# Float32 projection in fp32r halves: where the sum of two weight blocks is formed

## The chip, the cores and the metric

The kernel runs on one core of one Trainium2 chip. The metric is the device time of one execution in microseconds. Several runs are made, and their median counts. Besides, one execution is recorded by the hardware profiler; its trace says what each engine did at what time.

## The reference

One layer of a decoder trunk: a sequence of 1024 tokens with 2048 features each. A combined projection is followed by two groups of heads (sparse attention on a latent, and a chunked matrix memory), an output projection and a normalisation. The change lies in the combined projection. Cut to what matters:

```python
def reference(x, w_in, ..., w_out, ln_g, ln_b):
    ...
    proj = x @ w_in[l]                       # (1024, 2048) @ (2048, 7512), float32
    (q_a, c_kv, z_a, q_i, k_i, w_i, q_m, k_m, v_m, i_m, f_m, o_m, z_m) = jnp.split(proj, offs, axis=-1)
    ...
    y = jnp.concatenate([y_a, y_m], axis=-1) @ w_out[l]
    x = layer_norm(ALPHA * x + y, ln_g[l], ln_b[l])
```

## The kernel before

**Halves.** A float32 product is made of three matmuls of a shorter type (fp32r): each operand is split into a high part (a cast by ScalarE) and a low part (what is left, a subtraction by VectorE), and high times high, low times high and high times low are summed in PSUM.

**Seven products for eight.** The large part of the projection is not computed block by block. A product of two 2 x 2 block matrices is made of seven block products instead of eight. The blocks of the input X and sums of them are called a11, a12, a22, s1, s2, s3, s4; those of the weights b11, b21, b22 and the sums t1 to t4. With B(q, n) for the weight block of row half q (four k tiles of 128) and column n (128 columns), the code needs b11 = B(0, 0), b21 = B(1, 0), b22 = B(1, 1); t1 is made from B(0, 0) and B(0, 1); t2 is t1 and B(1, 1); t4 is t2 and B(1, 0); t3 is made from B(1, 1) and B(0, 1). (Signs are carried by the X sums and by the way in which results are added; the weight sums are plain additions here.)

**Units and passes.** Class `Unit` (from line 695) computes two column groups of 128 columns for all 1024 tokens. There are 20 units (NU), and the 2048 features are done in two passes of 1024: the first pass (second is False) stores its results in part_d, the second (second is True) loads them and adds. So there are 40 unit runs, each of seven products; a product is twelve matmuls of 128 x 512 (four k tiles, three matmuls each, line 754). A block of weights is 128 x 512 float32, 256 KB.

**The order around the change.** `unit(i, ...)` calls `begin` of the next unit (its product b11) ahead of `end` of this one (product t4); `middle` runs b21, t1, t2, b22, t3. In the code's order b11 of a unit is thus followed by t4 of the unit before, then b21 and t1; the first unit of a pass has no such t4. The planner of the build (a timeline simulation with its own estimates of costs) then places the instructions on the engines by priority; everything in `urgent()` has a raised priority. Each engine and each queue takes its instructions in the order that the planner wrote.

**Loads and buffers.** `Unit.load(q, n, more)` (line 715) takes a buffer wraw, starts a load of B(q, n) into it from the SP queue (line 720) and, where `more` names a second block, an accumulating load of it into the same buffer from POOL (line 723). It keeps the buffer in a dictionary under (q, n, more), so that a second request for the same key gives the same buffer. There are six wraw buffers (WR), four each for the high and low parts wh and wl (WB), shared by all users of those names. `weights(name)` (line 727) asks for the block, adds a second block on VectorE where needed (line 741), casts the high part on ScalarE (line 744) and subtracts the low part on VectorE (line 745). Before the change t1 is formed by its own pair of loads, under the key (0, 0, (0, 1)):

```python
                else:
                    src = self.load(0, 0, (0, 1))
                    if name != "t1":
                        vec.tensor_tensor(src, src, self.load(1, 1 if name == "t2" else 0), op=OP.add)
```

So t2 and t4 are formed in place in t1's buffer. A unit run loads five blocks over SP (b11, b21, t1's first, b22, t3's first) and two by accumulation over POOL (t1's and t3's second).

**What else runs beside the units.** In the first pass index matmuls (lines 577 and 578), their ScalarE and VectorE steps (579, 584) and a search for thresholds (615, 618); in the second pass the matrix memory (mLSTM), with a selection on POOL (line 996). PSUM results of a unit are added to the tile res by VectorE (line 763) or copied by ScalarE (765, 767).

Of the kernel before, what the change touches and what calls it, by code (L numbers as in the profile page):

```python
# [15 lines left out]
OP = mybir.AluOpType  # L16
# [86 lines left out]
def kernel(ctx, tc, a, out):  # L103
    nc = tc.nc
    vec, act, pool, pe, sync = nc.vector, nc.scalar, nc.gpsimd, nc.tensor, nc.sync
# [29 lines left out]
    def urgent():  # L135
        return tc.high_priority(offset=W_PRIO)
# [159 lines left out]
    class Queries:  # L296
# [3 lines left out]
        def run(self, p, again, X, between=lambda k: None):  # L300
# [35 lines left out]
            def product(ps, wname, xname, start, then):  # L336
                fh, fl = X[xname]
                for u in range(4):
                    wh, wl = weights(wname, u)
                    for k in range(4):  # L340
                        for n, (w, x) in enumerate(((wh, fh), (wh, fl), (wl, fh))):
                            last_mm[0] = pe.matmul(ps[u], w[:, k], x[:, k], start=start and k == 0 and n == 0,
                                                   stop=k == 3 and n == 2, skip_group_check=True)
                        if k % 2:
                            marks.append(last_mm[0])
                    then(u, ps[u])
# [326 lines left out]
    def search_on():  # L673

        if searching[0]:
            with tc.issue_after(last_cast[0].ins), tc.issue_after(last_low[0].ins):
                next(steps, None)
# [17 lines left out]
    class Unit:  # L695
# [31 lines left out]
        def weights(self, name):  # L727

            with urgent():
                if name == "b11":  # L730
                    src = self.load(0, 0)
                elif name == "b21":
                    src = self.load(1, 0)
                elif name == "b22":
                    src = self.load(1, 1)
                elif name == "t3":
                    src = self.load(1, 1, (0, 1))
                else:
                    src = self.load(0, 0, (0, 1))
                    if name != "t1":  # L740
                        vec.tensor_tensor(src, src, self.load(1, 1 if name == "t2" else 0), op=OP.add)  # L741
                wh = wp.tile([P, 4, P], F32R, name="wh", tag="wh", bufs=WB)
                wl = wp.tile([P, 4, P], F32R, name="wl", tag="wl", bufs=WB)
                last_cast[0] = act.copy(wh, src)  # L744
                last_low[0] = vec.tensor_tensor(wl, src, wh.bitcast(F32), op=OP.subtract)  # L745
            search_on()
            return wh, wl

# [66 lines left out]
    class Values:  # L815
# [11 lines left out]
        def run(self, second, X):  # L827
# [28 lines left out]
            def product(ps, wname, xname, start, group=4):  # L856
                fh, fl = X[xname]

                def part(t, k, w):
                    ts = slice(t * P, (t + 1) * P)  # L860
                    for n, (x, y) in enumerate(((fh, w[0]), (fl, w[0]), (fh, w[1]))):
                        last_mm[0] = pe.matmul(ps[t], x[:, k, ts], y, start=start and k == 0 and n == 0,
                                               stop=k == 3 and n == 2, skip_group_check=True)
                    if t % 2:
                        marks.append(last_mm[0])

                ws = {}
                for t0 in range(0, 4, group):
                    for k in range(4):
                        if not t0:  # L870
                            ws[k] = weights(wname, k)
                        for t in range(t0, t0 + group):
                            part(t, k, ws[k])
# [388 lines left out]
    with ExitStack() as ph:  # L1262
# [126 lines left out]
        for h in range(H_A):  # L1389
            qk = k_next + q_next  # L1390
            gt, tb = head_inputs(h) if h else head_0
            if h == 0:
                sync.dma_start(gt, gate_a[0])
            if h + 1 < H_A:
                k_next, q_next = keys(h + 1), queries(h + 1)
            order = range(4) if h < H_A - 1 else range(3, -1, -1)
            for n, p in enumerate(order):
                pr = weights(p, qk, tb)
                for step in y_steps.get(4 * h + n, ()):
                    y_step(*step)  # L1400
                consume(AHEAD - 1)
                if n == 0 and h % 2 == 0:
                    while blocks:
                        mix(blocks.pop(0))
                    values_of[h // 2] = values(h // 2)
                units.append((h, p, pr, gt, n == 3))
# [268 lines left out]
```

## Time and profile before

| | |
|---|---|
| median of 3 runs | 1823.08 us (1821.39 to 1825.92) |
| profiled execution | 1821.88 us |
| its span | 1820.1 us |
| TensorE busy (matmuls) | 1771.6 us, 97% |
| VectorE, ScalarE, GpSimd busy | 1398.2, 942.2, 267.7 us |
| loads of wg into wraw | 224 over SP, 80 over POOL |

In a row of the profile an engine has a short name: PE is TensorE (PEld its weight loads), DVE VectorE, ACT ScalarE, POOL GpSimd, SP SyncE; a q behind it (SPq) means its queue, which issues transfers and waits on semaphores. A group's row gives the line of the kernel, engine, operation, output<-inputs with shapes and xcount, then busy time and the mean in ns, then the idle time of the engine just before, and what ended most of it. A row of the timeline begins with start and duration in us; brackets at its end give the idle time before it and its releaser. A row of the waits gives, behind the two sides, the total in us, how many times, and the longest. A row of the stages begins with from:to, then the length in us, then each engine's busy time and instructions, the granted TensorE clock, the busy share of the DMA engines and GB/s. A DMA row gives KB each and the median us from issue to landing.

### The profile page before, as it was taken

The numbers are of one execution on the slowest core, as the hardware profiler recorded it, in microseconds if no ns is written. First come the engines' busy times: TensorE is split into PE (matmuls) and PEld (weight loads), VectorE is DVE, ScalarE is ACT, GpSimd is POOL, SyncE is SP. The second block draws the span as 40 slices with busy tenths as digits, with TensorE's granted clock in tenths as the row PEclk, the third lists the DMA queues.
The fourth block names the chain that finished last, engine by engine and source line by source line (L and its number), as shares of the span: only waits on it lengthen the run. The fifth ranks groups of instructions, "written<-read, shape, count | busy, mean of one in ns | idle before, by whom it ended". The sixth has DMA issues, their size and how long they took to land. (4 is left out here: it accounts for less than half of the span.)

```text
span 1820.1 us, 25472 instructions
## 1 busy us (share of the span) xinstructions
PE 1771.6 (97%) x8613; PEld 1492.9 (82%) x8613; DVE 1398.2 (77%) x2674; ACT 942.2 (52%) x1728; POOL 267.7 (15%) x324
## 2 busy tenths in 40 slices
PE   8999999999999999999999999999989999999997
PEld 8888888887888887788888887878788987788886
DVE  8756677767887768887878787877898976676787
ACT  6442266556666658322555565565665664333410
POOL 3101100000100010000101010010454530011000
PEclk9999999999999999999999999999999999999999
DMA  9994264445475657886766656475776447864764
GB/s 322 329 334 120 91 167 120 110 125 144 132 207 146 169 161 243 284 248 192 205 174 181 206 143 200 105 206 172 239 201 159 119 111 221 282 192 120 190 190 142
DMA packets 147069, 336.73 MB, mean 185 GB/s; under 512 B 15977, under 2 KB 25449, under 8 KB 140793
## 3 DMA queue, kind: packets, MB, share of 16 engines
q1 hardware_dynamic: 119576, 275.96, 45.8%
q0 software_dynamic: 27360, 59.13, 17.1%
q8 instruction: 68, 1.11, 0.2%
q14 instruction: 65, 0.52, 0.1%
HBM read 257.31 MB, written 91.35 MB: 192 GB/s over the span
## 5 line engine op out<-in xcount | busy, mean ns | idle before, releaser
L754 PE MATMUL pj<-xh,wh 128*128 128x512 f32 x960 | 375.8, 393 | 4.6 <-DVE res L763 3.8
L754 PE MATMUL pj<-xl,wh 128*128 128x512 f32 x960 | 374.9, 391 | 0.0
L754 PE MATMUL pj<-xh,wl 128*128 128x512 f32 x960 | 370.8, 391 | 0.6 <-DVE wl L745 0.6
L744 ACT CAST wh<-wraw 128x512 fp32r<-128x512 f32 x280 | 172.1, 619 | 203.0 <-PE pj L754 88.2
L745 DVE TENSOR_TENSOR wl<-wraw,wh 128x512 fp32r<-128x512 f32 x280 | 191.3, 687 | 46.6 <-ACT wh L744 40.9
L754 PEld LDWEIGHTS pj<-xh,wh 128*128 128x128 f32 x960 | 180.3, 188 | 43.0 <-ACT pqh L108 2.4
L754 PEld LDWEIGHTS pj<-xh,wl 128*128 128x128 f32 x960 | 180.1, 188 | 37.6 <-DVE wl L745 1.8
L754 PEld LDWEIGHTS pj<-xl,wh 128*128 128x128 f32 x960 | 180.4, 188 | 34.5
L723 POOL DMA_DIRECT2D wraw<-wg x80 | 68.1, 851 | 751.9 <-DMA wraw<-wg 254.5
L763 DVE TENSOR_TENSOR res<-res,pj 128x512 f32<-128x512 f32 x160 | 109.2, 682 | 53.7 <-PE pj L754 43.2
L584 DVE SCALAR_TENSOR_TENSOR sc<-r,wi,sc 128x384 f32<-128x384 f32 (+2 forms) x90 | 84.1, 948 | 30.9 <-ACT r L579 30.2
L579 ACT ACTIVATE r<-sc 128x384 f32<-128x384 f32 (+3 forms) x160 | 79.2, 523 | 52.3 <-PE sc L578 41.2
L615 ACT ACTIVATE junk<-sc,cand 128x512 bf16<-128x512 f32 (+2 forms) x93 | 86.7, 933 | 6.0 <-DVE cand L630 6.0
L108 ACT CAST wh<-wraw 128x512 fp32r<-128x512 f32 (+2 forms) x80 | 45.2, 571 | 70.4 <-PE lps L1487 22.0
L618 DVE TENSOR_SCALAR_CACHE_REDUCE junk<-sc,cand 128x384 bf16<-128x384 f32 (+2 forms) x93 | 80.0, 875 | 0.9
L1319 POOL TENSOR_TENSOR nm<-mask,tb 128x256 f32<-128x256 bf16 (+3 forms) x64 | 66.5, 1119 | 83.2 <-DVE mn L1326 76.8
L109 DVE TENSOR_TENSOR wl<-wraw,wh 128x512 fp32r<-128x512 f32 (+2 forms) x80 | 51.0, 642 | 30.3 <-ACT wh L108 28.6
L754 PE MATMUL pb<-xh,wh 128*128 128x512 f32 x160 | 62.9, 393 | 0.0
L754 PE MATMUL pb<-xh,wl 128*128 128x512 f32 x160 | 62.5, 391 | 0.0
L754 PE MATMUL pb<-xl,wh 128*128 128x512 f32 x160 | 62.4, 390 | 0.0
L1331 ACT ACTIVATE lg<-lg,mn 128x256 f32<-128x256 f32 (+3 forms) x64 | 50.4, 790 | 15.9 <-DVE mn L1326 15.9
L741 DVE TENSOR_TENSOR wraw<-wraw 128x512 f32<-128x512 f32 x80 | 55.0, 687 | 1.0
(562 smaller groups left out, 4476.6 us busy)
## 6 DMA issues: line engine op xcount, KB each, us to landing
wraw<-wg SPq DMA_DIRECT2D x224, 256.0 KB, 4.0
wraw<-wg POOLq DMA_DIRECT2D x80, 256.0 KB, 5.1
part_d<-res SPq DMA_DIRECT2D x20, 1024.0 KB, 5.1
res<-part_d SPq DMA_DIRECT2D x19, 1024.0 KB, 8.4
wraw<-wo SPq DMA_DIRECT2D x64, 256.0 KB, 4.6
wraw<-wv SPq DMA_DIRECT2D x48, 256.0 KB, 5.6
v_d<-v SPq DMA_DIRECT2D x16, 512.0 KB, 5.2
z<-x SPq DMA_DIRECT2D x16, 512.0 KB, 4.1
```

The source lines that it names most:

```text
L109: vec.tensor_tensor(lo, src, hi.bitcast(F32), op=OP.subtract)
L579: act.activation(r[:, s], ps, AF.Relu)
L584: vec.scalar_tensor_tensor(out=sc[t], in0=r, scalar=wcol, in1=sc[t], op0=OP.mult, op1=OP.add)
L615: act.activation(junk, sc[t], AF.Sign, scale=-1.0, bias=th[:, t - 2:t - 1], accum_out=cnt[:, t - 2:t - 1])
L618: vec.tensor_scalar(junk, sc[t], th[:, t - 2:t - 1], 0.0, op0=OP.is_lt, op1=OP.add, accum_out=cnt[:, t - 2:t - 1])
L723: pool.dma_start(r, a["wg"][self.g + more[1], :, k0:k0 + 4, :], accum_op=OP.add)
L741: vec.tensor_tensor(src, src, self.load(1, 1 if name == "t2" else 0), op=OP.add)
L744: last_cast[0] = act.copy(wh, src)
L745: last_low[0] = vec.tensor_tensor(wl, src, wh.bitcast(F32), op=OP.subtract)
L754: last_mm[0] = pe.matmul(ps, w[:, k], x[:, k], start=start and k == 0 and n == 0, stop=k == 3 and n == 2, skip_group_check=True)
L763: vec.tensor_tensor(dst, dst, ps, op=OP.subtract if minus else OP.add)
L1319: last_sum[0] = pool.tensor_tensor(nm[:, 0:ws], mask[t][:, w - ws:w], tb[:, off:off + ws], op=OP.add)
```

## The change

The block B(0, 0) of a unit run is loaded once. t1, t2 and t4 now ask for the same key as b11 and so get b11's buffer. Right behind the split of b11 (inside the same raised priority) POOL issues the accumulating load of B(0, 1) into that buffer; it must come after both reads of the buffer by the split, and t1's cast must wait for it. The loads of b21, b22 and t3 stay as they are. A unit run then loads four blocks over SP and two by accumulation over POOL. The buffer of b11 is held until t4's split, and t1 claims none of its own.

```diff
                 elif name == "t3":
                     src = self.load(1, 1, (0, 1))
                 else:
-                    src = self.load(0, 0, (0, 1))
+                    src = self.load(0, 0)
                     if name != "t1":
                         vec.tensor_tensor(src, src, self.load(1, 1 if name == "t2" else 0), op=OP.add)
                 wh = wp.tile([P, 4, P], F32R, name="wh", tag="wh", bufs=WB)
                 wl = wp.tile([P, 4, P], F32R, name="wl", tag="wl", bufs=WB)
                 last_cast[0] = act.copy(wh, src)
                 last_low[0] = vec.tensor_tensor(wl, src, wh.bitcast(F32), op=OP.subtract)
+                if name == "b11":
+                    k0 = 8 * self.second
+                    pool.dma_start(src, a["wg"][self.g + 1, :, k0:k0 + 4, :], accum_op=OP.add)
             search_on()
             return wh, wl
```

## The prediction

> **What bounds the kernel now.** I read the page first, then the busy time of each engine by stage, then the list of who waited for whom on TensorE, then the timeline of single units on each engine. The lines of the page that matter:
>
> ```profile
> span 1820.1 us, 25472 instructions
> ...
> PE 1771.6 (97%) x8613; PEld 1492.9 (82%) x8613; DVE 1398.2 (77%) x2674; ACT 942.2 (52%) x1728; POOL 267.7 (15%) x324
> ...
> q1 hardware_dynamic: 119576, 275.96, 45.8%
> ...
> L744 ACT CAST wh<-wraw 128x512 fp32r<-128x512 f32 x280 | 172.1, 619 | 203.0 <-PE pj L754 88.2
> L745 DVE TENSOR_TENSOR wl<-wraw,wh 128x512 fp32r<-128x512 f32 x280 | 191.3, 687 | 46.6 <-ACT wh L744 40.9
> ...
> wraw<-wg SPq DMA_DIRECT2D x224, 256.0 KB, 4.0
> wraw<-wg POOLq DMA_DIRECT2D x80, 256.0 KB, 5.1
> ```
>
> The profiled execution took 1821.88 us, 1.8 more than its span, and lies 1.2 under the median of the runs, 1823.08. TensorE is busy 97% of it, but busy rows of a pipelined engine overlap, so I look at the stages. The changed code runs in two of them: the first pass of the 20 units (about 215 to 660 us) and the second (about 830 to 1270).
>
> ```profile
> core 0: us, PE busy (x) PEld busy (x) DVE busy (x) ACT busy (x) POOL busy (x), PEclk, DMA share, GB/s
> 0.00:215.00 215.00, 207.89 (x1021) 182.72 (x1022) 151.17 (x268) 89.86 (x157) 33.92 (x60) 0.99 0.73 246
> 215.00:660.00 445.00, 443.11 (x1998) 367.69 (x1997) 340.38 (x640) 285.97 (x579) 39.96 (x50) 1.00 0.53 145
> 660.00:740.00 80.00, 78.80 (x348) 64.79 (x347) 63.26 (x132) 51.46 (x93) 6.84 (x8) 1.00 0.77 235
> 740.00:830.00 90.00, 86.02 (x370) 69.74 (x369) 74.48 (x118) 25.70 (x41) 8.56 (x10) 0.98 0.84 263
> 830.00:1270.00 440.00, 435.09 (x2095) 362.03 (x2094) 341.21 (x628) 246.97 (x398) 41.52 (x46) 1.00 0.62 178
> 1270.00:1470.00 200.00, 184.99 (x1245) 166.99 (x1244) 176.31 (x440) 125.76 (x258) 98.77 (x106) 1.00 0.60 174
> ```
>
> In the two passes TensorE is idle 1.9 and 4.9 us; the DMA engines are busy 53% and 62%, so they do not bound them. How close the matmuls stand, and what a product costs, the timeline of TensorE in the first pass says (tile pb is written only by the product of block b21):
>
> ```profile
> 581.88 0.39 PE L754 MATMUL pb<-xh,wh 128*128 128x512 f32 x1
> 582.11 0.39 PE L754 MATMUL pb<-xl,wh 128*128 128x512 f32 x1
> ...
> 584.38 0.39 PE L754 MATMUL pb<-xh,wl 128*128 128x512 f32 x1
> 584.60 0.39 PE L754 MATMUL pj<-xh,wh 128*128 128x512 f32 x1
> ```
>
> A matmul starts every 0.227 us, and the twelve of a product take 2.72 us, at the full granted clock (1.00 in both stages). So the passes run at the rate of TensorE, and only what makes TensorE wait costs time. Over the whole kernel its waits at the units' line are these:
>
> ```profile
> PE pj L754 <- DVE res L763: 3.8, 4, 2.0
> ...
> PE pj L754 <- ACT wh L744: 0.9, 2, 0.6
> ...
> PE pj L754 <- DVE wl L745: 0.6, 1, 0.6
> ```
>
> That is 5.3 us in all, of which 1.5 are for weights (the cast wh and the low part wl). By 0.3% of the time, about what a measurement here can tell from no change, I mean 5.5 us. So even if every wait at the changed code's matmuls went, it would not reach that bound.
>
> **What goes.** Each of the 40 unit runs loads four blocks over SP and not five. That is 40 of the 224 SP loads of wg: 40 x 256 KB = 10.5 MB of the 275.96 MB of that queue, in proportion 1.7 points of its 45.8% share. No wait of TensorE in the passes is for a DMA, so I cost this at nothing; what hides it is the matmul stream itself. The change also asks for four of the six wraw buffers per unit instead of five. SP stands long before these loads because buffers are not free:
>
> ```profile
> SPq L720 <- DVE wraw L741: 280.1, 37, 14.5
> ```
>
> ScalarE's own waits for a loaded block all lie in the first pass:
>
> ```profile
> ACT wh L744 <- DMA wraw<-wg: 17.3, 7, 6.0
> ```
>
> Seven of them, 17.3 us together, and TensorE lost at most the 0.9 us above. I credit half of the 1.5 us of weight waits to earlier loads: -0.7, between 0 and -1.5.
>
> **What is added.** The number of accumulating loads (two per unit) and their queue stay. But the one for t1 no longer follows an SP load made in advance: it must wait until ScalarE's cast and VectorE's subtract of b11 have read the buffer. The new chain is: cast 0.62, subtract 0.69, a hand-off to POOL that I put at 0.5 (an estimate, as no row singles it out), then the accumulate. Its time from issue to landing comes from line 723's own view:
>
> ```profile
> DMA to landing us min/median/max: 4.1/5.1/13.2
> ```
>
> So 0.62 + 0.69 + 0.5 + 5.1 = 6.9 us from the start of b11's cast until t1's cast can start. In the code's order two products, t4 of the unit before and b21, lie between b11 and t1, so three cast intervals. On ScalarE the casts in the densest part come like this:
>
> ```profile
> 573.70 0.62 ACT L744 CAST wh<-wraw 128x512 fp32r<-128x512 f32 x1 [0.44 <-PE pj L754]
> ...
> 576.42 0.62 ACT L744 CAST wh<-wraw 128x512 fp32r<-128x512 f32 x1 [0.47 <-PE pj L754]
> ...
> 579.14 0.62 ACT L744 CAST wh<-wraw 128x512 fp32r<-128x512 f32 x1 [0.22 <-PE pj L754]
> ```
>
> One per product, 2.72 us apart, each released by the matmuls that give back one of the four wh buffers. Three intervals are 8.2 us, so the 6.9 fit with 1.3 to spare, and wherever index or mLSTM matmuls stand between, with more. There is a second cover behind it. With four buffers a cast runs three products ahead: the one at 573.70 is for the product whose matmuls begin at 581.88, 8.2 us later. Less its own 0.62, TensorE feels a late cast only after another 7.5 us. So an accumulate may land 5.1 + 1.3 + 7.5 = 13.9 us after issue before TensorE waits; the slowest of the 80 took 13.2. One late block of the trace shows it:
>
> ```profile
> 524.22 0.62 ACT L744 CAST wh<-wraw 128x512 fp32r<-128x512 f32 x1 [3.59 <-DMA wraw<-wg]
> ```
>
> ScalarE stood 3.59 us there for such a load, and the list of TensorE's waits between 505 and 545 us is empty. I cost the steady units at nothing.
>
> The cover is missing at one place in each pass, its first unit: no t4 stands between, and b11, b21, t1 follow one another.
>
> ```profile
> 226.67 0.98 POOL L723 DMA_DIRECT2D wraw<-wg  x1
> ...
> 227.56 0.69 DVE L745 TENSOR_TENSOR wl<-wraw,wh 128x512 fp32r<-128x512 f32 x1
> ...
> 233.64 0.62 ACT L744 CAST wh<-wraw 128x512 fp32r<-128x512 f32 x1 [2.17 <-DMA wraw<-wg]
> ...
> 234.38 0.43 PE L754 MATMUL pj<-xh,wh 128*128 128x512 f32 x1
> ```
>
> ```profile
> 836.71 1.29 DVE L745 TENSOR_TENSOR wl<-wraw,wh 128x512 fp32r<-128x512 f32 x2
> ...
> 837.64 0.39 PE L754 MATMUL pj<-xh,wh 128*128 128x512 f32 x1
> ```
>
> The first four rows are the start of the first pass, the other two that of the second. First pass: today's accumulate is issued at 226.67, ahead of the subtract, and the cast waits for it until 233.64, 7.0 us. After the change it is issued at 227.56 + 0.69 + 0.5 = 228.75. With the median 5.1 t1's matmuls could start at 228.75 + 5.1 + 0.62 = 234.5, 0.1 late; with the 7.0 that this very place shows, at 236.4, 2.0 late. I take 2.0. Second pass: the two subtracts at 836.71 share 1.29, so b11's ends near 837.4; the accumulate lands at 837.4 + 0.5 + 5.1 = 843.0 and t1 can start at 843.6. TensorE has b11 and b21 until 837.64 + 24 x 0.227 = 843.1: 0.5 late. Together +2.5. The bounds: 0 if both land in 4.1, and 2 x (13.2 - 5.1) more, about +17, if both take as long as the slowest.
>
> Behind the waiting accumulate POOL holds t3's accumulate, needed two or more products later, and in the second pass the selection on ri:
>
> ```profile
> POOL ri L996 <- DMA ri<-rows_d: 22.4, 7, 6.2
> ```
>
> POOL already stands 22.4 us there for a transfer, without a row of TensorE's waits for it; and it is busy only 41.52 of the 440 us. Nothing more is charged.
>
> At one place a rule of the Trainium skill can be set against the rows. "DMA: Bandwidth & Descriptors", section "Anatomy of one DMA — SWDGE (gpsimd) path", gives a DMA from GpSimd about 2.0 us fixed plus bytes at 436 GB/s; for 256 KB that makes, as an estimate, 2.6 us, and the start of both passes would then cost nothing. The trace has 5.1 for these accumulates, so the trace decides.
>
> **Sum.** 1821.9 + 2.5 - 0.7 = 1823.7 on the profiled execution's own time, and 1.2 more by the median: 1824.9, no change that can be told.
>
> **Rivals.** *The accumulate comes last after all (slower).* ScalarE takes its work in order; if it stops at t1's cast in every unit, the evictions and casts behind it are late too, and the three products of lead are never won back. It decides from the point where an accumulate lands later than 13.9 us after issue, or from 6.4 if the lead is already gone. Its price from a row: the two waits of TensorE for a cast are 0.45 us each; in 38 units 17 us, so 1824.9 + 17 = 1842. Against it stand the 5.1 and the 524 us row. For it: VectorE is busy 341 of 440 us, so subtracts come late at times. In "DMA: Bandwidth & Descriptors", section "Rules for kernel authors", the Trainium skill says to issue a DMA early and wait for it late; this change issues one later. By that rule the time would be this rival's; the trace so far does not bear it out, as late landings cost TensorE nothing.
>
> *The freed buffer decides (faster).* With four claims instead of five SP runs ahead, and the 5.3 us of unit waits go, with some of the 4.0 us idle of the stage 740 to 830, whose loads stand behind in the same queue: between 1823.1 - 9.3 = 1813.8 and 1818.4, half of it. Against it: the larger part, 3.8, is for VectorE's additions, which wait on no load.
>
> *The order is laid out anew.* A planner at build time places every instruction by estimated times. 40 loads fewer and a new dependency can shift orders throughout, also in stages that the change does not touch. TensorE's idle time outside the passes is 7.1 + 1.2 + 4.0 + 15.0 = 27.3 us (four stages above). Moved by a third, a choice of mine, this is 9 us either way: 1814 or 1832. No row speaks for a side.
>
> That the loads do not go can be excluded from the code: t1, t2 and t4 now ask for the block that b11 has already stored under the same key.
>
> **Chances.** The forecast 0.66, of which 0.05 above the bound (a long landing at a pass start); late accumulates 0.09; freed buffer 0.10, half of it within the bound; new order 0.15, 0.10 of it slower. So faster 0.05 + 0.05 = 0.10, slower 0.05 + 0.09 + 0.10 = 0.24, the rest, 0.66, within. The range runs from 1817 to 1833: it takes in the slower new order, most of the long landings and half the freed buffer's gain, and leaves out late accumulates above and 1814 below, under 2 in 10.
>
> **What would show it.** Right: 184 SP loads of wg, 80 accumulates, TensorE's waits at line 754 still about 5 us, idle time in both passes within a few us, and POOL's wait at line 723 for wl of b11 grown. Wrong by the first rival: waits of ScalarE for a loaded block far above 17.3 us, and TensorE's waits for wh above 5 us. Wrong by the second: TensorE's waits at line 754 gone. Wrong by the third: idle time that appears or goes in stages before 215 or after 1270 us.

## The result, and the profile after

The changed kernel takes 1851.01 us (median of 4 runs, 1847.79 to 1851.6), the kernel before in the same comparison 1822.32 (4 runs, 1821.39 to 1825.92). The ratio is 1.0147, with a 95% interval from 1.0134 to 1.016: slower, the medians 28.7 us apart, and outside the predicted range of 1817 to 1833. The profiled execution took 1850.95 us, 1.75 more than its span.

The page of the changed kernel, at the lines that answer to those shown of before (the units' matmuls are now line 757, the result addition 766, and the new accumulate 748):

```profile
span 1849.2 us, 25422 instructions
...
PE 1786.0 (97%) x8613; PEld 1500.8 (81%) x8613; DVE 1395.9 (75%) x2674; ACT 939.9 (51%) x1727; POOL 266.7 (14%) x324
...
q1 hardware_dynamic: 113816, 265.47, 43.4%
...
L744 ACT CAST wh<-wraw 128x512 fp32r<-128x512 f32 x280 | 172.0, 619 | 223.0 <-PE pj L757 77.3
L745 DVE TENSOR_TENSOR wl<-wraw,wh 128x512 fp32r<-128x512 f32 x280 | 191.2, 686 | 78.0 <-ACT wh L744 76.5
...
wraw<-wg SPq DMA_DIRECT2D x184, 256.0 KB, 3.6
wraw<-wg POOLq DMA_DIRECT2D x80, 256.0 KB, 5.8
```

The loads went as intended: 184 over SP instead of 224, 10.5 MB less on that queue. The matmuls are the same 8613. What grew is TensorE's idle time (span less busy time: 48.5 to 63.2 us), its busy time for the same matmuls (1771.6 to 1786.0), and the median landing of the accumulates, 5.1 to 5.8 us. The last section comes back to the busy time. The stages say where (columns as before; the passes now lie at about 215 to 675 and 850 to 1290):

```profile
215.00:675.00 460.00, 453.83 (x2032) 373.15 (x2032) 342.90 (x650) 288.48 (x585) 39.28 (x50) 1.00 0.48 130
...
850.00:1290.00 440.00, 423.20 (x2005) 350.73 (x2004) 327.47 (x609) 240.46 (x389) 40.82 (x46) 0.98 0.56 156
```

In its two passes TensorE is idle 6.2 and 16.8 us, against 1.9 and 4.9 before, and in the second the granted clock is 0.98 instead of 1.00. Measured from the start of the first to the end of the last matmul at the units' line, the first pass takes 463.2 us instead of 455.8, the second 462.5 instead of 441.5. The three other stages agree within 0.7 us. So the loss is 7.4 + 21.0 us, nearly all of the 29.1 by which the spans differ, and it lies in the two passes that hold the changed code. The waits (engine and work, what it waited for: us in total, times, longest):

```profile
POOL wraw L748 <- DVE wl L745: 185.5, 19, 22.7
POOL wraw L723 <- DMA wraw<-wg: 115.5, 10, 21.1
...
ACT wh L744 <- DMA wraw<-wg: 61.5, 16, 8.3
...
PEld pj L757 <- ACT wh L744: 18.8, 12, 4.0
...
PE pj L757 <- ACT wh L744: 13.9, 9, 3.5
```

ScalarE waits 61.5 us for a loaded block (17.3 before), and TensorE 13.9 us for a cast (0.9 before). Both are the signs that the prediction gave for its first rival. The view of line 748, with who waited for it and its times from issue to landing, names the accumulate:

```profile
  ACT wh L744: 57.7, 14
...
DMA to landing us min/median/max: 4.1/6.1/11.0
```

57.7 of the 61.5 us are for it. It comes last; the question is why. One place of the timeline, all engines, rows of other work left out (the matmul at 926.30 is needed further below):

```profile
922.01 0.69 DVE L745 TENSOR_TENSOR wl<-wraw,wh 128x512 fp32r<-128x512 f32 x1
922.69 0.87 POOL L723 DMA_DIRECT2D wraw<-wg  x1 [15.25 <-DVE wl L745]
923.25 1.19 POOL L748 DMA_DIRECT2D wraw<-wg  x1
923.99 0.62 ACT L744 CAST wh<-wraw 128x512 fp32r<-128x512 f32 x1 [0.24 <-PE pj L757]
...
926.30 0.39 PE L757 MATMUL pj<-xl,wh 128*128 128x512 f32 x1
...
932.65 0.62 ACT L744 CAST wh<-wraw 128x512 fp32r<-128x512 f32 x1 [8.04 <-DMA wraw<-wg]
...
933.32 0.50 PE L757 MATMUL pj<-xh,wh 128*128 128x512 f32 x1 [3.06 <-ACT wh L744]
```

An accumulate of line 723, t3's, goes out just ahead of the new one of line 748, and t1's cast stands 8.04 us for the block. The order in which the planner wrote POOL's queue shows that this is no chance: before the change t1's accumulate is ahead of t3's in all 40 unit runs. After it, in 29 of the 40 (counted over both passes from 0: 9 to 11, 13 to 20, 22 to 39) t3's stands ahead of the new one. The order of casts on ScalarE is the same in both kernels: b11 of the next unit, t4, b21, t1, t2, b22, t3.

### The profile page after: what moved, and what is told of

Same layout as the page of the kernel before. It is cut to its first block, busy times and chain, and to the rows that moved or that the text cites. A ratio compares the mean times of both kernels' runs of the same rounds, so it can differ in the third digit from the quotient of the medians.

```text
span 1849.2 us, 25422 instructions
## 1 busy us (share of the span) xinstructions
PE 1786.0 (97%) x8613; PEld 1500.8 (81%) x8613; DVE 1395.9 (75%) x2674; ACT 939.9 (51%) x1727; POOL 266.7 (14%) x324
## 4 chain that ended last, share of the span: by engine, by line
PE 34%; DVE 7%; DMA 6%; issue 2%; ACT 1%; POOL 0%; SPq 0%; DVEq 0%; ACTq 0%; POOLq 0%
PE pj L757 10%; PE lps L1490 6%; PE pc L1490 2%; PE pb L757 1%; DMA wraw<-wg 1%; PE lps L112 1%; PE lps L113 1%; PE lps L114 1%; PE pb L1490 1%; PE tps L1354 1%; DMA vraw<-v_d 1%; DMA ri<-rows_d 1%; DVE lg L1337 1%; DMA wraw<-y_d 1%; PE zps L112 1%
## 5 line engine op out<-in xcount | busy, mean ns | idle before, releaser
L757 PE MATMUL pj<-xh,wh 128*128 128x512 f32 x960 | 380.7, 397 | 15.4 <-ACT wh L744 13.9
L723 POOL DMA_DIRECT2D wraw<-wg x40 | 34.5, 862 | 523.8 <-DMA wraw<-wg 115.5
L748 POOL DMA_DIRECT2D wraw<-wg x40 | 38.2, 954 | 206.0 <-DVE wl L745 185.5
```

The source lines that it names most:

```text
L757: last_mm[0] = pe.matmul(ps, w[:, k], x[:, k], start=start and k == 0 and n == 0, stop=k == 3 and n == 2, skip_group_check=True)
```

## The experiments

**Theory 1, the order on POOL.** POOL takes its queue in order. t3's accumulate waits for its own SP load, which in turn waits for a free buffer. Where it stands ahead, t1's accumulate is held behind it although b11's split is done; then both go out within 0.6 us of each other and land later than one alone. **Rival: the late issue itself** (an accumulate that may start only behind the split is too late, wherever it stands), or the shared buffer.

All runs below but the first are compared with runs of the kernel before on the same chip: 1825.38 us (17 runs) for the first four, 1825.19 (30 runs) for the others.

**1. Names only.** The changed kernel, its buffers named by block and its high parts by product (rawA for b11's and t1's buffer, rawD for t3's, whta for t1's high part), nothing else.

```diff
-                r = wp.tile([P, 4, P], F32, name="wraw", tag="wraw", bufs=WR)
+                r = wp.tile([P, 4, P], F32, name="raw" + BLOCK[q, n, bool(more)], tag="wraw", bufs=WR)
...
-                wh = wp.tile([P, 4, P], F32R, name="wh", tag="wh", bufs=WB)
+                wh = wp.tile([P, 4, P], F32R, name="wh" + KIND[name], tag="wh", bufs=WB)
```

> The changed kernel with names that tell the blocks (rawA for B(0, 0), rawB, rawC, rawD for t3's) and the products (whba for b11, whta for t1 and so on) apart; every engine's order of instructions is the same as in the changed kernel, so the time should be 1847 to 1852 us. It is for reading. Theory 1 (the POOL queue: in 29 of the 40 unit runs the planner put t3's accumulate ahead of the one behind b11's split, and that one then stands behind a wait for t3's own SP load): b11's split ends several us before its accumulate is issued, and the issue follows t3's within 1 us. Theory 2 (the wait on the split itself is too long): the accumulate is issued within 1 us of the end of the split, and still lands after t1's cast could have begun.

One run: 1856.8 us, 31 above the median of before on that chip and some 5 above what was expected. The engines' orders are those of the changed kernel. The timeline around the worst unit run:

```profile
1031.48 0.33 SPq L720 DMA_DIRECT2D rawD<-wg  x1
...
1033.06 0.60 ACT L744 CAST whba<-rawA 128x512 fp32r<-128x512 f32 x1
1033.69 0.69 DVE L745 TENSOR_TENSOR wlba<-rawA,whba 128x512 fp32r<-128x512 f32 x1
...
1037.60 0.87 POOL L723 DMA_DIRECT2D rawD<-wg  x1 [17.18 <-ACT sh L108]
...
1038.17 1.18 POOL L748 DMA_DIRECT2D rawA<-wg  x1
...
1048.08 0.62 ACT L744 CAST whta<-rawA 128x512 fp32r<-128x512 f32 x1 [9.45 <-DMA rawA<-wg]
...
1048.75 0.80 PE L757 MATMUL pj<-xh,whta 128*128 128x512 f32 x1 [3.99 <-ACT whta L744]
```

The split of b11 is done at 1033.69 + 0.69 = 1034.38. The new accumulate goes out at 1038.17, right behind t3's, whose SP load had been issued only at 1031.48. A free accumulate goes 0.30 us after the subtract (the median of the 40); here it is held 3.8 us, and it lands 9.8 us after issue. (The releaser printed for POOL, a ScalarE step, is only inferred.) In 11 of the unit runs the hold is over 1 us, up to 4.65; in these 11 the new accumulate takes a median 8.8 us to land.

**2. b11's accumulate first.** The changed kernel with an order, and no wait, on POOL: t3's accumulate is queued behind the new one of its unit.

```diff
-                    pool.dma_start(r, a["wg"][self.g + more[1], :, k0:k0 + 4, :], accum_op=OP.add)
+                    with tc.issue_after(self.acc.ins):
+                        pool.dma_start(r, a["wg"][self.g + more[1], :, k0:k0 + 4, :], accum_op=OP.add)
...
-                    pool.dma_start(src, a["wg"][self.g + 1, :, k0:k0 + 4, :], accum_op=OP.add)
+                    self.acc = pool.dma_start(src, a["wg"][self.g + 1, :, k0:k0 + 4, :], accum_op=OP.add)
```

> The changed kernel, with one edge for the planner: on POOL, t3's accumulate of a unit run comes behind the one behind b11's split. Loads, buffers and the wait on the split stay. Theory 1 (order on the POOL queue): 1820 to 1828 us, ScalarE's waits for a loaded block back from 61 to about 20 us. Theory 2 (the wait on the split itself): 1843 to 1852 us. Theory 3 (other shifts of the planner's order): anywhere between, with the idle time of TensorE outside the two passes changed.

1829.2 us, ratio 1.0019 (1.0004 to 1.0035), a little above the expected range. One edge in the order takes back all but 0.19% of the 1.47%, with the late issue and the shared buffer left as they are. The passes take 455.2 and 445.6 us. In the first pass POOL's queue is all that changed: row by row, SP, TensorE, ScalarE and VectorE take the same instructions in the same order as in run 1, whose order is the changed kernel's (so too in runs 5 and 6). The pass takes 8.0 us less than in the changed kernel and 11.7 less than in run 1. In the second pass the planner also laid out the other engines anew (about 500 of TensorE's 2111 rows stand elsewhere), so what came back there is not shown to be POOL's order alone. The new accumulate is never held for more than 1 us. A rest is left, since t3's still follows about half a microsecond behind in the denser units:

```profile
ACT whta L745 <- DMA rawA<-wg: 34.5, 13, 6.1
```

**3. The wrong order put into the kernel before.** Five loads, t1's own buffer, no wait for a split; only t3's accumulate is queued ahead of t1's on POOL in the 29 unit runs in which the changed kernel has it so. The order of the weight blocks' SP loads stays as it was.

```diff
                 if more:
                     k0 = 4 * (more[0] + 2 * self.second)
-                    pool.dma_start(r, a["wg"][self.g + more[1], :, k0:k0 + 4, :], accum_op=OP.add)
+                    behind = q == 0 and self.i + 20 * self.second in D_FIRST
+                    if behind:
+                        self.load(1, 1)
+                        self.load(1, 1, (0, 1))
+                    with tc.issue_after(self.acc.ins) if behind else ExitStack():
+                        self.acc = pool.dma_start(r, a["wg"][self.g + more[1], :, k0:k0 + 4, :], accum_op=OP.add)
```

> The kernel before, five SP loads per unit run and no wait on the split, but in the same 29 unit runs t3's accumulate is put ahead of t1's on POOL. Theory 1: it becomes slower, 1838 to 1860 us, and ScalarE waits for t1's block in those units. Theory 2: no change, 1818 to 1828 us, as nothing waits for the split.

1894.44 us, ratio 1.0391 (1.0366 to 1.0415), more than was expected: the order turned, without anything else of the change, costs more than the change does. (Here too the planner moved other instructions, few in the first pass, 12 of TensorE's 2034 rows, and many in the second. The passes take 484.4 and 483.3 us.)

```profile
POOL rawD L729 <- DMA rawD<-wg: 177.6, 18, 20.9
ACT whta L750 <- DMA rawS<-wg: 141.9, 29, 10.0
...
PE pj L760 <- ACT whta L750: 37.0, 17, 4.9
```

POOL stands 177.6 us for t3's SP load with t1's accumulate (rawS is t1's buffer here) behind it, and ScalarE waits 141.9 us for t1's block, 10.0 at the longest.

**4. Only one accumulate left.** The changed kernel, but t3's B(0,1) comes by a plain SP load and VectorE adds it.

```diff
                 elif name == "t3":
-                    src = self.load(1, 1, (0, 1))
+                    src = self.load(0, 1)
+                    vec.tensor_tensor(src, src, self.load(1, 1), op=OP.add)
```

> The changed kernel, with t3's sum formed otherwise: B(0, 1) is loaded plainly over SP and VectorE adds B(1, 1), so that b11's accumulate is the only one of a unit run on POOL; 40 additions of 0.69 us, 27 us, come onto VectorE. Theory 1: 1818 to 1830 us (nothing stands ahead of the accumulate; the additions are hidden). Theory 2: 1843 to 1855 us, since the wait on the split is the same. If VectorE is close to setting the pace, up to 10 us more under either.

1849.89 us, ratio 1.0133 (1.0116 to 1.015). Theory 1 missed by some 20 us: with nothing ahead on POOL the kernel is as slow as the changed one. The waits and VectorE's timeline show the same fault in another queue:

```profile
DVE rawE L738 <- DMA rawE<-wg: 31.7, 24, 3.0
```

```profile
1035.43 0.69 DVE L738 TENSOR_TENSOR rawE<-rawE,rawC 128x512 f32<-128x512 f32 x1 [2.26 <-DMA rawE<-wg]
1036.04 0.42 DVE L1089 COPY state<-up 128x258 f32<-128x258 f32 x1
1036.38 0.68 DVE L746 TENSOR_TENSOR wlba<-rawA,whba 128x512 fp32r<-128x512 f32 x1
```

The planner put t3's addition ahead of b11's subtract (wlba), and VectorE, which is in order too, stood there for the load of rawE. b11's cast had begun at 1032.97; the subtract ends at 1037.06, 4.1 us later, and the accumulate goes out at 1037.36. That is only a reading so far; run 8 tests it.

**5. t3's accumulate left out.** No addition in its place: t3 is split from B(1,1) alone, so B(0,1) is missing from that sum.

```diff
                 sync.dma_start(r, a["wg"][self.g + n, :, k0:k0 + 4, :])
-                if more:
-                    k0 = 4 * (more[0] + 2 * self.second)
-                    pool.dma_start(r, a["wg"][self.g + more[1], :, k0:k0 + 4, :], accum_op=OP.add)
```

> The changed kernel with t3's accumulating load left out (t3 is split from B(1,1) alone, so B(0,1) is missing from that sum); the new accumulate behind b11's split is the only one of the units on POOL, and VectorE gets no addition in its place. Theory of the POOL queue (t3's accumulate stands ahead of the new one and holds it): the new one goes 0.3 us behind the subtract in every unit, lands alone in 4 to 6 us, the first pass takes 443 to 446 us, the second 434 to 441, the whole 1815 to 1826. Rival (an accumulate that may start only behind the split is late by itself, whatever stands ahead of it, which would fit the run with one accumulate at 1849.9): ScalarE's waits for its block stay above 40 us, and the time 1840 to 1850.

1824.67 us, ratio 0.9999 (0.9987 to 1.001). The new accumulate, issued just as late and into the same shared buffer, costs the whole run nothing that can be told when POOL has nothing ahead of it. The rival of the late issue falls.

**6. t3's accumulate waits for t1's cast.** Like run 2, but a real wait, so that the two are never in flight together.

```diff
-                    pool.dma_start(r, a["wg"][self.g + more[1], :, k0:k0 + 4, :], accum_op=OP.add)
+                    d = pool.dma_start(r, a["wg"][self.g + more[1], :, k0:k0 + 4, :], accum_op=OP.add)
+                    tc.add_manual_dep(d.ins, self.t1.ins.name, mybir.DependencyInfo(
+                        mybir.DependencyClass.Sync, mybir.DependencyReason.DATA), reason="t3 behind t1")
...
                 last_low[0] = vec.tensor_tensor(wl, src, wh.bitcast(F32), op=OP.subtract)
+                if name == "t1":
+                    self.t1 = last_cast[0]
```

> The changed kernel with a real wait of t3's accumulate for t1's cast of the same unit, so that the new accumulate is always ahead and never shares its flight with t3's. Theory (what was left over in the run with b11's accumulate first, 34.5 us of ScalarE's waits and 0.2%, came from two accumulates in flight within half a microsecond): t1's landing 4 to 6 us in dense units too, ScalarE's waits for t1's block below 20 us, 1818 to 1827, equal to before or a little faster. Rival (the held accumulate comes late for t3, or stands ahead of the next unit's new one): waits of ScalarE for t3's block appear, above 20 us, and the time is 1830 to 1845.

1825.81 us, ratio 1.0002 (0.9989 to 1.0015): the whole change, with all its sums, as fast as before. (In the one profile of the run the first pass takes 455.2 us, 0.6 less than before, but the second 445.9, 4.4 more, made up by shorter stages ahead of the passes; runs 2, 5 and 8 have 445.6 to 447.0 in the second. Whether some 4 us are left there was not settled.)

```profile
POOL rawD L723 <- ACT whta L746: 183.7, 28, 11.1
...
ACT whta L746 <- DMA rawA<-wg: 27.8, 11, 6.1
...
ACT whtc L746 <- DMA rawD<-wg: 2.9, 2, 1.6
```

POOL now stands 183.7 us at t3's accumulate, as long as the 185.5 us at line 748 of the changed kernel, and that costs nothing that can be told: nothing urgent is queued behind. t3's own cast waits 2.9 us. In the 11 unit runs that were held in run 1 the new accumulate now lands in a median 5.3 us, not 8.8, with the hold 5.8 after the split, not 10.3. Over all 40, by that line's own view:

```profile
DMA to landing us min/median/max: 4.1/5.0/10.2
```

ScalarE's waits came to 27.8 us, above the 20 expected: in a few dense units an accumulate takes over 8 us even alone, and run 5 has the same 27.6. These TensorE does not feel.

**7. The change in the first pass only.**

```diff
-                    src = self.load(0, 0)
+                    src = self.load(0, 0) if not self.second else self.load(0, 0, (0, 1))
...
-                if name == "b11":
+                if name == "b11" and not self.second:
```

> The change in the first pass alone; the second loads t1's pair as before, with t1's accumulate ahead of t3's on POOL in all its units. Theory of the POOL queue: the first pass takes 450 to 456 us as in the changed kernel (it still has units with t3's accumulate first), the second 436 to 439 as before, the whole 1828 to 1834. Rival (buffers, or an order laid out anew in the whole kernel): the second pass is above 445 us too, the whole above 1840.

1833.57 us, ratio 1.0043 (1.0026 to 1.0059). In its profiled execution, 6 us above its median, the first pass takes 466.9 us, 11.1 more than before, and the second 442.8, 1.3 more. (The lengths in the expectations of runs 5 and 7 are about 11 us lower for the first pass and 5 for the second than from first to last matmul; the differences to before are not touched by that.) In the second pass, where t1's accumulate is ahead on POOL again, the time is back.

**8. Run 4 with VectorE's addition moved back.** The addition for t3 is queued behind t1's subtract.

```diff
                     src = self.load(0, 1)
-                    vec.tensor_tensor(src, src, self.load(1, 1), op=OP.add)
+                    with tc.issue_after(self.t1.ins):
+                        vec.tensor_tensor(src, src, self.load(1, 1), op=OP.add)
...
                 last_low[0] = vec.tensor_tensor(wl, src, wh.bitcast(F32), op=OP.subtract)
+                if name == "t1":
+                    self.t1 = last_low[0]
```

> The run with one accumulate (t3's B(0,1) loaded plainly and added by VectorE), but VectorE's addition queued behind t1's subtract of the same unit instead of ahead of b11's. Theory (in that run VectorE, which takes its work in order, stood at the addition for the load, 31.7 us in 24 places, and b11's subtract behind it, so that the new accumulate was released late): b11's subtract ends about 2 us after the start of its cast in every unit, ScalarE's waits for t1's block below 30 us, 1820 to 1830. Rival (40 more additions of 0.69 us on VectorE and 40 more loads are the cost by themselves): 1840 to 1850 again.

1826.39 us, ratio 1.0005 (0.9994 to 1.0016). The loads and additions of run 4, 40 of each, are all still there; only their place differs, and 23 us are gone. Run 4's miss was the order again, on another engine.

ScalarE's wait for t1's block and the time, against before on the same chip, run by run:

| run | ScalarE waits for t1's block, us | time against before, us |
|---|---|---|
| 8, 5, 6 | 27.4, 27.6, 27.8 | +1.2, -0.5, +0.6 |
| 2 | 34.5 | +3.8 |
| 7 | 42.0 | +8.4 |
| 4 | 58.0 | +24.5 |
| 1 (one run) | 79.6 | +31.4 |
| 3 | 141.9 | +69.1 |

With some 27 us of these waits the time is that of before. What lies above goes with lost time, though not in a fixed proportion.

## Why the prediction was wrong

**The step that failed** is the one that ends "Behind the waiting accumulate POOL holds t3's accumulate, needed two or more products later ... Nothing more is charged." It asked what the new accumulate would hold up, and took the order on POOL as given. It did not ask what the planner would put ahead of it. Runs 2, 3 and 6 show that this order makes the loss: without it 1829.2 and 1825.8, with it put into the kernel before 1894.4. In the first pass, where the other engines' orders are those of the changed kernel, it is 8.0 us of 463.2. The warning stood in the profile before, in a row of the waits that the prediction did not read:

```profile
POOL wraw L723 <- DMA wraw<-wg: 254.5, 29, 24.6
```

POOL already stood 254.5 us at accumulates whose SP load had not landed. That was harmless only as long as t1's was not behind them.

**The chain of the steady units** was sized well, for an accumulate that is free to go. The hand-off is 0.30 us (estimated 0.5), the landing alone a median 5.0 us in run 6 (5.1). "I cost the steady units at nothing" holds there.

**The limit of 13.9 us** failed as well. It counted from the issue, and so left out the time before it. No landing of line 748 in the changed kernel passed it, 11.0 us was the longest, and still TensorE waited. Its 7.5 us of lead were also too much. They were read off a cast for b21, three products ahead, and t1 has less, because TensorE does not take the products in the order of the code or of the casts: in 28 of the 38 unit runs that follow another in their pass, t1's product goes ahead of the t4 that was to stand between (28 in run 1, 28 in run 6). In run 6 t1's cast ends a median 2.8 us before TensorE comes to its product. The place at 932.65 shows it. t1's cast takes the high-part buffer that t3's matmuls give back, and the last of these, at 926.30 in the timeline above, ended at 926.69. (In run 6 the cast of the same unit run starts just as t3's matmul ends.) With its block there the cast could have begun then, and its matmuls 0.67 later, at 927.36; TensorE stood ready from 933.32 - 3.06 = 930.26. The lead there was 2.9 us.

**The two pass starts**, +2.5 us, were right: t1's first matmuls show idle times of 1.97 (predicted 2.0) and 0.70 us (predicted 0.5).

```profile
235.77 0.50 PE L757 MATMUL pj<-xh,wh 128*128 128x512 f32 x1 [1.97 <-ACT wh L744]
```

```profile
851.58 0.50 PE L757 MATMUL pj<-xh,wh 128*128 128x512 f32 x1 [0.70 <-ACT wh L744]
```

**What goes** was right in that it gains nothing: 40 loads fewer, and the best of the variants (runs 5, 6 and 8) stand within 0.1% of before. The -0.7 for earlier loads cannot be told apart from nothing.

**The rivals.** The first named the symptom, the side and nearly the size (1842, which was luck) but not the cause: TensorE waited for a cast 9 times, up to 3.5 us, not 38 times 0.45, and because the accumulate was held and shared its flight, not because it was issued behind the split. The third, an order laid out anew, comes nearest to the true cause, but the prediction looked for it in stages that the change does not touch and gave it 9 us either way; it sat in POOL's queue, right beside the change. (Its 27.3 us of idle time outside the passes also leave out the last 350 us of the span, where TensorE was idle for another 14.3.) In the prediction the Trainium skill's rule from "DMA: Bandwidth & Descriptors", section "Rules for kernel authors", issue early and wait late, stood beside the first rival. Run 6 issues as late and loses nothing, so here it was not the late issue that decided.

**Still open.** Why the planner brought t3's accumulate forward was only argued: with one buffer less claimed, t3's load can be placed earlier. And the passes lost unequally. ScalarE's waits for a block in the first pass and in the second:

```profile
ACT wh L744 <- DMA wraw<-wg: 41.1, 12, 5.4
```

```profile
ACT wh L744 <- DMA wraw<-wg: 20.4, 4, 8.3
```

The first lost 7.4 us with 41.1 us of them, the second 21.0 with 20.4. Some of the second's loss may be TensorE's own order, which the planner turned there too (run 2). Another part is a late transfer of another kind: TensorE's longest interval, 3.93 us between two matmul starts at 1232, follows a wait of ScalarE for mLSTM's ri, whose load stood on SP behind two wraw loads.

```profile
1219.44 8.72 SPq L720 DMA_DIRECT2D wraw<-wg  x2
1228.22 0.43 SPq L998 DMA_DIRECT2D ri<-rows_d  x1
```

In the SP order of the changed kernel this load stands one wraw load later than in run 2 or 6. It was not tried by itself. The clock has its part as well, below.

## What to carry to other kernels

When a change makes a queued step wait for something new, read its queue in both directions: what stands behind it, and what the planner may now place ahead of it that waits for a transfer of its own. A long wait of an in-order queue costs nothing until something urgent is queued behind the step that waits, so look for such rows before the change and ask what would happen if the urgent step landed there. An explicit order between the two, one line, is cheaper to write than to find out.

## What the hardware did that was not expected

**A wait of 3 us costs more than 3 us.** The changed kernel around the wait at 930 us (from:to, length, busy time and count of PE, PEld, DVE, ACT, POOL, the granted clock, DMA share, GB/s):

```profile
927.00:933.00 6.00, 3.26 (x19) 2.53 (x17) 0.64 (x1) 0.35 (x1) 0.00 (x0) 1.00 0.73 240
933.00:936.00 3.00, 2.68 (x8) 2.17 (x9) 1.72 (x4) 2.97 (x5) 0.00 (x0) 0.72 0.02 5
936.00:939.00 3.00, 3.00 (x14) 2.46 (x14) 2.29 (x4) 1.23 (x3) 0.00 (x0) 0.71 0.00 0
939.00:942.00 3.00, 3.00 (x15) 2.49 (x14) 2.06 (x3) 2.99 (x5) 0.00 (x0) 1.00 0.45 120
```

After the wait the granted clock is 0.72 and 0.71 over the next 6 us: seven matmuls start 0.43 us apart instead of 0.227, and the steps beyond 0.227 add up to 1.7 us on top. At the four intervals over 2.7 us between matmul starts in the second pass, such steps add 0.9 to 2.6 us each, about 7 together; before the change the granted clock was 1.00 throughout both passes. The Trainium skill, "TensorE: Matmul & The Clock Gate", section "Why this matters for your kernels", says to leave no gaps over about 3 us between bursts of matmuls, or the clock falls back. The trace agrees in the main: it fell after idle times of 2.80, 3.06 and 3.54 us. But it also fell after one of 2.37 (at 1138.51) and one of 1.95 (at 707.99), and not after one of 2.49 in run 6 (at 1115.82) or 2.02 in the kernel before (at 1109.53).

**Two accumulates close together.** In ten of the 11 held unit runs of run 1 the two accumulates went out within 0.6 us of each other. The second, the new one, took a median 8.8 us to land in those 11, against 5.3 in the same unit runs of run 6, where it went alone.
